# First down projection of a decoder trunk: two of its seven block products in the wide form, and their additions moved between engines

## The chip, the core and the metric

The program runs on one core of a Trainium2 chip. Five engines work side by side, each in the order in which its instructions were written: TensorE (PE in the profile, with its weight loads as PEld) multiplies, VectorE (DVE) and ScalarE (ACT) work element by element, GpSimd (POOL) here mostly issues transfers that add to what lies at the destination, and SyncE (SP) issues plain transfers. They wait for one another by semaphores. The metric is the device time of one execution in microseconds, as a median of several runs.

## The reference

The reference is one decoder layer on 512 tokens of 1024 channels, in float32:

```python
x = x + 0.5 * swiglu(rmsnorm(x, ffn1_norm), ffn1_wg, ffn1_wu, ffn1_wd)
x = x + hybrid_mixer(rmsnorm(x, mix_norm), w_in, ...)
x = x + 0.5 * swiglu(rmsnorm(x, ffn2_norm), ffn2_wg, ffn2_wu, ffn2_wd)
return rmsnorm(x, final_norm)

def swiglu(x, w_gate, w_up, w_down):
    return (silu(x @ w_gate) * (x @ w_up)) @ w_down     # 1024 -> 2816 -> 1024
```

The change lies in the first of the three lines, in its last matrix product: the hidden values (2816 by 512 tokens) times `w_down` (2816 by 1024), scaled by one half and added to x. The mixer (sparse attention beside a gated recurrence) and the second feed-forward are as before.

## The kernel before

Values lie transposed: channels over the 128 partitions, tokens along a row. A float32 operand is split in two tiles that TensorE takes at its fast rate: a rounded one, written by ScalarE, and the remainder (value minus rounded value), written by VectorE. A product w times t is then three matmuls: rounded w by rounded t, rounded w by remainder of t, remainder of w by rounded t. For weights the tiles are called `wh` and `wl`; for operands `ch` and `cl`.

The down projections are done by blocks with seven products in place of eight (the scheme of Strassen and Winograd). The 22 hidden tiles make 11 pairs: ten pairs lie in five tiles `a` and `b` of two hidden tiles each (`ha_103`, `hb_104` and so on in the profile, numbered n = 0 to 4), and the last pair is called "joined" (j = 10, operands `cx`). With tokens halved (`lo`, `hi`, 256 columns each) and output channels halved (four tiles of 128, m = 0 to 3), each of the seven products takes sums or differences of blocks on both sides. The order of the work is the list `steps` in `block_down`, 78 steps: the joined steps of products 1 and 2, product 1, product 2, product 5 and its joined step, product 6, product 3, product 7, product 4. A group in the text below is one n of a product, two steps, that is 16 pairs of (k tile, m).

Around each step hangs a table of tasks, keyed by the step's number: `unit` splits the weights of two steps (one ScalarE and one VectorE instruction of 1024 columns), `operand` splits the operand, `difference` makes a(hi) - b(hi) for product 7 (it is needed from step 23 on), `reduced` turns a(hi) into a(hi) - a(lo) by a ScalarE copy with the sign turned and a transfer of GpSimd that adds it, and `joined_sum` adds weight blocks of the joined pair. Weights of products 1, 2 and 4 come from memory into three raw buffers `wr` (a load can start when VectorE has read the buffer), those of the other products into `sm`, `s` and `sj`, to which GpSimd's transfers add further blocks. Since every engine runs its own list in order, a task that is listed late or waits holds up all that stands behind it on that engine.

PSUM, where TensorE's sums build up, has eight banks of 512 columns, in two tags of four: `mm` and `aux`. Products 1, 6, 7 and 4 add up in `mm`, one bank for each m, of which product 1 and 6 use all 512 columns and 7 and 4 the lower 256. Product 2 uses two `aux` banks, two m in a bank; products 5 and 3 share two others in the same way.

Products 1 and 6 (the constant `BROAD`) take the wide form: the operand tile holds the rounded values in its lower 256 columns and the remainder in its upper 256, so the two matmuls with the rounded weights are one of 512 columns, and the third one of 256 adds to the lower half. Per m and k tile these are two matmuls in place of three. The upper half of the bank has to be added at the end (`results1`). The operand takes two ScalarE and two VectorE instructions of 256 columns in place of one each of 512.

`results1(i)` adds a finished product's banks to x by one VectorE instruction of 256 columns for each m (`result1`). The tables are set by hand in steps; a later stage of the program has its order chosen by a planner (`Plan`). Line 251 in the profile is the helper that issues all arithmetic instructions, line 239 the one that issues transfers.

## Time and profile before

| | us |
|---|---|
| median of 3 runs | 1036.72 (1036.44 to 1037.26) |
| the profiled execution | 1036.25 |
| its span, first to last instruction | 1034.5 |
| TensorE busy in the span | 1027.6 (99%) |
| VectorE busy | 906.6 (88%) |
| ScalarE busy | 710.4 (69%) |
| GpSimd busy | 203.3 (20%) |
| granted TensorE clock | 0.999 |

The stage of the change lies from about 226 to 337 us of the span. By stretches of it: the first product without its joined step takes 13.97 us of TensorE, the second 14.40, the fifth and the third 15.84 each with their joined steps, the sixth 15.40. A time stands in us from the span's start. VectorE's and ScalarE's instructions are pipelined: a row's duration is longer than the distance to the next row's start, and where work is added up below, that distance is used.

### The profile page before, as it was taken

Reading aid. Unit: us, or ns where it says so; the run is one execution under the profiler, and the core shown is the slowest. Engines: PE = TensorE matmul, PEld = TensorE weight load, DVE = VectorE, ACT = ScalarE, POOL = GpSimd, SP = SyncE. Lnnn points to the kernel's source line nnn. Section 1 sums busy time; section 2 is a strip of 40 time slices with the busy share of each in tenths; the row PEclk is TensorE's granted clock in tenths of the full one; section 3 lists DMA queues with packets and bytes.
Section 4 is the critical chain, followed back from the end, with each engine's and each line's share of the span. In section 5 each row is a group of like instructions: output and inputs, shape, how many; then the busy total and the mean of one; then the engine's idle time right before and its main releaser. Section 6 shows DMA issues by size and latency. Waiting matters only on the chain.

```text
span 1034.5 us, 16004 instructions
## 1 busy us (share of the span) xinstructions
PE 1027.6 (99%) x5600; PEld 892.9 (86%) x5600; DVE 906.6 (88%) x1571; ACT 710.4 (69%) x1195; POOL 203.3 (20%) x255
## 2 busy tenths in 40 slices
PE   9999999999999999999999999999999999999997
PEld 8898888899999888888888888888988888898886
DVE  7988999889998888998989966777889999989886
ACT  8856766666766669978896674367666766657864
POOL 1613333213240011111101110013432333110000
PEclk9999999999999999999999999999999999999999
DMA  9969999897994463343469987793889999987564
GB/s 355 201 171 216 222 238 216 192 275 194 183 244 152 149 181 101 107 128 107 122 187 282 278 212 209 208 295 62 193 226 245 215 221 227 205 203 225 167 189 164
DMA packets 92257, 206.01 MB, mean 199 GB/s; under 512 B 18576, under 2 KB 25872, under 8 KB 92176
## 3 DMA queue, kind: packets, MB, share of 16 engines
q1 hardware_dynamic: 59952, 141.75, 41.0%
q0 software_dynamic: 31936, 62.93, 35.0%
q8 instruction: 44, 0.72, 0.3%
q10 hardware_dynamic: 288, 0.31, 0.1%
q14 instruction: 37, 0.30, 0.1%
HBM read 185.02 MB, written 25.17 MB: 203 GB/s over the span
## 4 chain that ended last, share of the span: by engine, by line
PE 99%; DVE 0%; DVEq 0%; issue 0%
PE mm L251 72%; PE aux L251 27%; PE aux L1340 0%; DVE xr L251 0%; DVE o L251 0%; DVE sq L251 0%; DVEq L2568 0%; DVE rs L251 0%; DVE ss L251 0%
## 5 line engine op out<-in xcount | busy, mean ns | idle before, releaser
L251 DVE TENSOR_TENSOR wl<-wr,wh 128x1024 fp32r<-128x1024 f32 (+3 forms) x154 | 183.0, 1189 | 30.6 <-ACT wh L251 30.1
L251 ACT ACTIVATE wh<-wr 128x1024 fp32r<-128x1024 f32 (+2 forms) x155 | 158.8, 1026 | 43.4 <-PE mm L251 20.0
L251 PE MATMUL mm<-cm,wh 128*128 128x512 f32 (+1 forms) x736 | 167.0, 354 | 0.0
L251 PEld LDWEIGHTS mm<-cm,wh 128*128 128x128 f32 x736 | 126.3, 190 | 15.8
L251 PE MATMUL mm<-yn,wh 128*128 128x512 f32 x420 | 130.8, 393 | 0.0
L251 PE MATMUL aux<-cm,wh 128*128 128x512 f32 (+1 forms) x472 | 119.5, 383 | 0.0
L251 PE MATMUL mm<-cm,wl 128*128 128x256 f32 x608 | 108.3, 282 | 0.0
L251 PEld LDWEIGHTS aux<-cm,wh 128*128 128x128 f32 x472 | 86.0, 188 | 15.6
L251 PEld LDWEIGHTS mm<-cm,wl 128*128 128x128 f32 x608 | 92.2, 190 | 4.7
L251 PEld LDWEIGHTS mm<-yn,wh 128*128 128x128 f32 x420 | 77.0, 188 | 14.8
L251 PE MATMUL mm<-yn,wl 128*128 128x512 f32 x210 | 81.9, 390 | 0.0
L251 PE MATMUL aux<-cm,wl 128*128 128x256 f32 x456 | 70.5, 282 | 0.0
L251 ACT ACTIVATE wh<-a 128x1024 fp32r<-128x1024 f32 (+1 forms) x68 | 57.1, 842 | 18.2 <-DVE a L251 17.2
L251 DVE TENSOR_TENSOR wl<-a,wh 128x1024 fp32r<-128x1024 f32 (+1 forms) x68 | 64.7, 952 | 5.5 <-ACT wh L251 5.0
L251 PE MATMUL mm<-yh,wh 128*128 128x512 f32 (+1 forms) x168 | 65.4, 392 | 0.0
L251 PE MATMUL mm<-yl,wh 128*128 128x512 f32 (+1 forms) x168 | 65.3, 390 | 0.0
L251 PEld LDWEIGHTS aux<-cm,wl 128*128 128x128 f32 x456 | 63.1, 191 | 1.9
L251 PE MATMUL mm<-yh,wl 128*128 128x512 f32 x160 | 62.1, 390 | 0.0
L251 ACT ACTIVATE tu<-mm 128x512 f32<-128x512 f32 (+1 forms) x57 | 28.2, 495 | 43.8 <-PE mm L251 43.7
L251 DVE TENSOR_TENSOR wl<-s,wh 128x1024 fp32r<-128x1024 f32 (+1 forms) x46 | 49.3, 1080 | 1.2 <-ACT wh L251 1.1
L251 ACT ACTIVATE wh<-s 128x1024 fp32r<-128x1024 f32 (+1 forms) x46 | 43.0, 943 | 7.1 <-PE mm L251 2.0
L251 PEld LDWEIGHTS mm<-yn,wl 128*128 128x128 f32 x210 | 39.4, 188 | 8.5
(400 smaller groups left out, 2596.8 us busy)
## 6 DMA issues: line engine op xcount, KB each, us to landing
wr<-wm SPq DMA_DIRECT2D x39, 512.0 KB, 3.6
w<-w2d SPq DMA_DIRECT2D x20, 512.0 KB, 7.0
wr<-w SPq DMA_DIRECT2D x20, 512.0 KB, 3.5
wr<-w1u SPq DMA_DIRECT2D x19, 512.0 KB, 5.9
s<-w2u SPq DMA_DIRECT2D x36, 256.0 KB, 4.4
wr<-w2u SPq DMA_DIRECT2D x18, 512.0 KB, 5.6
s<-w2u POOLq DMA_DIRECT2D x36, 256.0 KB, 6.3
s<-w1u SPq DMA_DIRECT2D x32, 256.0 KB, 4.8
```

Source lines behind the costliest of these rows:

```text
L251: return call(*args, **kw)
```

## The change

1. Products 5 and 3 take the wide form too (`BROAD`). They now have four `aux` banks, one for each m, and with that no bank is left beside the two of product 2: the banks of m = 2 and 3 are those that product 2 has to give back first. The first group of product 5 is therefore written in halves, m = 0, 1 for both of its steps and then m = 2, 3, and product 2's additions to x are listed ahead of it. Products 5 and 3 each need four more additions at their end (the upper halves). Product 5's and 3's operands are split by instructions of 256 columns.
2. `difference`, in this projection only, is a ScalarE copy of b(hi) with the sign turned and a transfer of GpSimd that adds a(hi); it was one VectorE subtraction. There are five.
3. The four `joined_sum` additions are listed at steps 12, 14, 16 and 18 (they were at 20 to 23).

```diff
--- before.py
+++ after.py
@@ -49,7 +49,7 @@
 PLAIN1, PAIRS1, TAIL, PLAIN2, PAIRS2, TAIL2 = 2, 10, 3, 2, 10, 4
 DIRECT, BEGIN = 2, 14
 SUMS_AT = -12, -11, -7, -5, -2
-BROAD = (1, 6)
+BROAD = (1, 6, 5, 3)
 WIDE, FIRST_FOLD = (2, 5, 3), 3
 KEPT, TURN = 6, 20
 MERGES = {(0, 0): 4, (1, 0): 7, (2, 1): 12, (3, 1): 16, (2, 0): 34, (3, 0): 36, (0, 1): 50, (1, 1): 54}
@@ -1117,7 +1117,11 @@
 
         def difference(n):
             ra[n] = two(slot(F32, "cr"))
-            V.tensor_sub(ra[n], a(n, hi), b(n, hi))
+            if made:
+                V.tensor_sub(ra[n], a(n, hi), b(n, hi))
+            else:
+                A.activation(ra[n], b(n, hi), AF.Copy, scale=-1.0)
+                G.dma_start(ra[n], a(n, hi), accum_op=ALU.add)
 
         def reduced(n):
             if made:
@@ -1195,7 +1199,7 @@
 
             for at, row in ((-9, 0), (-8, 1), (3, 2), (5, 3)):
                 task(at, [("SP", 0.6, lambda row=row: joined_load(row), False)])
-            for at, o, m, n in ((20, "w5", 2, 3), (21, 2, 2, 0), (22, 0, 0, "w5"), (23, 1, 1, 0)):
+            for at, o, m, n in ((12, "w5", 2, 3), (14, 2, 2, 0), (16, 0, 0, "w5"), (18, 1, 1, 0)):
                 task(at, lambda o=o, m=m, n=n: joined_sum(o, m, n))
 
         used = []
@@ -1492,17 +1496,18 @@
     broads1 = {}
 
     def chain1(p, m):
-        if CHAIN.get(p, p) == 1:
-            return broad1(m)[:, lo]
+        if p in BROAD or CHAIN.get(p, p) == 1:
+            return broad1(p, m)[:, lo]
         key = CHAIN.get(p, p), m // 2
         if key not in banks1:
             banks1[key] = psum("aux")
         return banks1[key][:, (lo, hi)[m % 2]]
 
-    def broad1(m):
-        if (1, m) not in broads1:
-            broads1[1, m] = psum()
-        return broads1[1, m]
+    def broad1(p, m):
+        key = CHAIN.get(p, p), m
+        if key not in broads1:
+            broads1[key] = psum("aux" if key[0] == 5 else "mm")
+        return broads1[key]
 
     def products1(i, ms=range(KD // 2)):
         if steps[i] is None:
@@ -1514,8 +1519,8 @@
             t = d1.turned[p, j]
             for m in ms:
                 c = slice(m * P, (m + 1) * P)
-                T.matmul(broad1(m), h[:, c], d1.whole[p], start=i == firsts1[1], stop=False, **opens)
-                T.matmul(broad1(m)[:, lo], l[:, c], t[0], start=False, stop=False, **opens)
+                T.matmul(broad1(p, m), h[:, c], d1.whole[p], start=i == firsts1[1], stop=False, **opens)
+                T.matmul(broad1(p, m)[:, lo], l[:, c], t[0], start=False, stop=i == lasts1[p], **opens)
             return
         if p in BROAD:
             h, l = d1.units[i // 2]
@@ -1524,9 +1529,9 @@
                 for m in ms:
                     c = slice(n % 2 * S + m * P, n % 2 * S + (m + 1) * P)
                     if j % 2 == 0:
-                        T.matmul(broad1(m), h[:, c], t, start=False, stop=False, **opens)
+                        T.matmul(broad1(p, m), h[:, c], t, start=p == 5 and n == 0, stop=False, **opens)
                     else:
-                        T.matmul(broad1(m)[:, lo], l[:, c], t[:, lo], start=False, stop=n == PAIRS1 - 1, **opens)
+                        T.matmul(broad1(p, m)[:, lo], l[:, c], t[:, lo], start=False, stop=n == PAIRS1 - 1 == lasts1[p] - i + j, **opens)
             return
         th, tl = d1.turned[p, j]
         for m in ms:
@@ -1550,13 +1555,13 @@
                     if st[0] == 6:
                         seconds = work("sq") if m % 2 == 0 else seconds
                         half_ = seconds[:, (lo, hi)[m % 2]]
-                        A.activation(half_, broad1(m)[:, hi], AF.Copy)
-                        V.tensor_add(broad1(m)[:, lo], half_, broad1(m)[:, lo])
+                        A.activation(half_, broad1(1, m)[:, hi], AF.Copy)
+                        V.tensor_add(broad1(1, m)[:, lo], half_, broad1(1, m)[:, lo])
                     result1(st[0], m, *a)
-                    if st[0] == 1:
+                    if st[0] in (1, 5, 3):
                         s_, half, sign = a
                         r = x[half * KD // 2 + m][:, (lo, hi)[s_]]
-                        V.scalar_tensor_tensor(r, broad1(m)[:, hi], 0.5 * sign, r, op0=ALU.mult, op1=ALU.add)
+                        V.scalar_tensor_tensor(r, broad1(st[0], m)[:, hi], 0.5 * sign, r, op0=ALU.mult, op1=ALU.add)
 
     def norm_round(k, c):
 
@@ -1587,14 +1592,17 @@
         plan.clear()
         cs = decay()
         turn_ = lasts1[7]
+        fifth_ = firsts1[5]
         for i in range(last):
-            if i in (turn_ - 1, turn_ + 1):
+            if i == fifth_:
+                results1(i - 1)
+            if i in (turn_ - 1, turn_ + 1, fifth_):
                 for ms in ((0, 1), (2, 3)):
-                    for k in (0, 1) if i < turn_ else (0, 2):
+                    for k in (0, 2) if i == turn_ + 1 else (0, 1):
                         products1(i + k, ms)
-            elif i not in (turn_, turn_ + 3):
+            elif i not in (turn_, turn_ + 3, fifth_ + 1):
                 products1(i)
-            if i and i - 1 != turn_:
+            if i and i - 1 not in (turn_, fifth_ - 1):
                 results1(i - 1)
             if i == turn_:
                 results1(i)
```

TensorE has 88 matmuls fewer, VectorE 13 instructions more, ScalarE 15 more, GpSimd five transfers more; SyncE's list is the same, and behind the projection the order on every engine is as before.

Where product 5 begins, TensorE had this before (`aux_2986` and `aux_2993` are the banks of product 5, m = 0 and 1 share the first; `ch` and `cl` the operand's rounded part and remainder, `wh` and `wl` those of the weights):

```order
L251 MATMUL aux_2986<-ch_2907,wh_2926 128x256
L251 MATMUL aux_2986<-cl_2908,wh_2926 128x256
L251 MATMUL aux_2986<-ch_2907,wl_2927 128x256
L251 MATMUL aux_2986<-ch_2907,wh_2926 128x256
L251 MATMUL aux_2986<-cl_2908,wh_2926 128x256
L251 MATMUL aux_2986<-ch_2907,wl_2927 128x256
```

and has this now (`aux_3003`, `aux_3005`, `aux_3013`, `aux_3015` are the banks of m = 0 to 3; `ch_2916` and `cl_2917` are the two k tiles of the group, each with both parts):

```order
L251 MATMUL aux_3003<-ch_2916,wh_2938 128x512
L251 MATMUL aux_3005<-ch_2916,wh_2938 128x512
L251 MATMUL aux_3003<-cl_2917,wh_2938 128x512
L251 MATMUL aux_3005<-cl_2917,wh_2938 128x512
L251 MATMUL aux_3003<-ch_2916,wl_2939 128x256
L251 MATMUL aux_3005<-ch_2916,wl_2939 128x256
L251 MATMUL aux_3003<-cl_2917,wl_2939 128x256
L251 MATMUL aux_3005<-cl_2917,wl_2939 128x256
L251 MATMUL aux_3013<-ch_2916,wh_2938 128x512
L251 MATMUL aux_3015<-ch_2916,wh_2938 128x512
L251 MATMUL aux_3013<-cl_2917,wh_2938 128x512
L251 MATMUL aux_3015<-cl_2917,wh_2938 128x512
```

Three matmuls of 256 columns became one of 512 and one of 256, ordered by halves of m; the ninth row is the first that needs a bank of product 2.

VectorE from the end of product 1's additions to x (`x<-mm`) to the weights of product 5 (`wl` from `sm`), before (`wl` from `wr` are the remainders of product 2's weights, groups 2, 3 and 4; `cl` are operands' remainders):

```order
L251 SCALAR_TENSOR_TENSOR x_95<-mm_2617,x_95 128x256 x2
L251 SCALAR_TENSOR_TENSOR x_95<-mm_2620,x_95 128x256 x2
L251 TENSOR_TENSOR wl_2822<-wr_2742,wh_2821 128x1024
L251 TENSOR_TENSOR cl_2838<-hb_110,ch_2837 128x512
L251 TENSOR_TENSOR wl_2857<-wr_2770,wh_2856 128x1024
L251 TENSOR_TENSOR cl_2873<-hb_112,ch_2872 128x512
L251 TENSOR_TENSOR wl_2892<-wr_2796,wh_2891 128x1024
L251 TENSOR_TENSOR cl_2908<-ha_103,ch_2907 128x512
L251 TENSOR_TENSOR wl_2927<-sm_2399,wh_2926 128x1024
L251 TENSOR_TENSOR cl_2943<-ha_105,ch_2942 128x512
L251 TENSOR_TENSOR sj_2959<-sj_2680,sj_2712 128x512
L251 TENSOR_TENSOR wl_2965<-sm_2408,wh_2964 128x1024
```

and now (`sj` are the joined sums, the pairs `ch_2916`, `cl_2917` the wide operand of product 5):

```order
L251 SCALAR_TENSOR_TENSOR x_95<-mm_2617,x_95 128x256 x2
L251 SCALAR_TENSOR_TENSOR x_95<-mm_2620,x_95 128x256 x2
L251 TENSOR_TENSOR sj_2823<-sj_2682,sj_2715 128x512
L251 TENSOR_TENSOR wl_2829<-wr_2746,wh_2828 128x1024
L251 TENSOR_TENSOR cl_2845<-hb_110,ch_2844 128x512
L251 TENSOR_TENSOR sj_2682<-sj_2682,sj_2448 128x512
L251 TENSOR_TENSOR wl_2865<-wr_2775,wh_2864 128x1024
L251 TENSOR_TENSOR cl_2881<-hb_112,ch_2880 128x512
L251 TENSOR_TENSOR sj_2448<-sj_2448,sj_2823 128x512
L251 TENSOR_TENSOR wl_2901<-wr_2801,wh_2900 128x1024
L251 TENSOR_TENSOR ch_2916<-ha_103,ch_2916 128x256
L251 TENSOR_TENSOR cl_2917<-ha_103,cl_2917 128x256
```

A joined sum stands ahead of each of product 2's last three weight remainders, and an operand of product 5 is two instructions of 256 columns.

ScalarE at the start of product 1, before (`wh` are rounded weights of product 1, `ch` and `cl` there the wide operands):

```order
L251 ACTIVATE tg_2360<-tg_2360 128x512
L251 ACTIVATE wh_2625<-wr_2519 128x1024
L251 ACTIVATE ch_2629<-ha_107 128x256
L251 ACTIVATE cl_2630<-ha_107 128x256
L251 ACTIVATE wh_2662<-wr_2552 128x1024
L251 ACTIVATE ch_2666<-ha_109 128x256
L251 ACTIVATE cl_2667<-ha_109 128x256
```

and now (`cr` are the differences for product 7):

```order
L251 ACTIVATE tg_2360<-tg_2360 128x512
L251 ACTIVATE cr_2623<-hb_104 128x512
L251 ACTIVATE wh_2626<-wr_2519 128x1024
L251 ACTIVATE ch_2630<-ha_107 128x256
L251 ACTIVATE cl_2631<-ha_107 128x256
L251 ACTIVATE cr_2661<-hb_106 128x512
L251 ACTIVATE wh_2664<-wr_2552 128x1024
L251 ACTIVATE ch_2668<-ha_109 128x256
L251 ACTIVATE cl_2669<-ha_109 128x256
```

One copy of 512 columns was put ahead of each weight of product 1. GpSimd's list in the same place:

```order
 L239 DMA sm_2516<-w1d 128x1024
+L239 DMA cr_2623<-ha_103 128x2x256
 L239 DMA sm_2574<-w1d 128x1024
-L239 DMA ha_103<-cr_2818 128x2x256
-L239 DMA ha_105<-cr_2853 128x2x256
-L239 DMA ha_107<-cr_2888 128x2x256
-L239 DMA ha_109<-cr_2923 128x2x256
+L239 DMA cr_2661<-ha_105 128x2x256
+L239 DMA cr_2694<-ha_107 128x2x256
+L239 DMA cr_2727<-ha_109 128x2x256
```

Five adding transfers of 128 by 512 values stand ahead of the five of `reduced` (`ha<-cr`); the first of them stands ahead of the last addition to product 5's weights (`sm_2574`).

## The prediction

> **What bounds the kernel now.** I read the busy times of the page first, then the chain of work that ended last, cut to the stretch of this projection, then the engines' rows in order of time around it.
>
> ```profile
> span 1034.5 us, 16004 instructions
> PE 1027.6 (99%) x5600; PEld 892.9 (86%) x5600; DVE 906.6 (88%) x1571; ACT 710.4 (69%) x1195; POOL 203.3 (20%) x255
> ```
>
> TensorE bounds the whole: 6.9 us of the span are not its own. So an edit pays only what it takes off TensorE's list, and costs whatever TensorE comes to wait for. The chain's pieces (start, us, count):
>
> ```profile
> 229.69 13.97 PE mm L251 x80
> 243.66 30.24 PE aux L251 x252
> 273.90 15.40 PE mm L251 x88
> 289.30 15.84 PE aux L251 x132
> 953.47 72.09 PE mm L251 x318
> ```
>
> The second row is products 2 (120 matmuls) and 5 (132), the third is the sixth in the wide form, the fourth is the third product. 30.24 / 252 = 0.120 us for a matmul of 256 columns, start to start; the last row gives 72.09 / 318 = 0.2267 us for 512 columns. There is no gap in products 2, 5 and 3, so TensorE waits for nothing there now. Product 2 runs from 243.66 to 258.06, product 5 to 273.90. A group of product 2 takes 24 x 0.120 = 2.88 us; its third group starts at 249.42.
>
> VectorE in the same stretch (start, us, idle before):
>
> ```profile
> 224.62 0.68 DVE L251 TENSOR_TENSOR cr<-ha,hb 128x512 f32<-128x512 f32 x1
> 243.05 1.23 DVE L251 TENSOR_TENSOR wl<-wr,wh 128x1024 fp32r<-128x1024 f32 x1 [1.23 <-ACT wh L251]
> 244.19 0.68 DVE L251 TENSOR_TENSOR cl<-hb,ch 128x512 fp32r<-128x512 f32 x1
> 244.79 3.24 DVE L251 SCALAR_TENSOR_TENSOR x<-mm,x 128x256 f32<-128x256 f32 x8
> 247.95 1.22 DVE L251 TENSOR_TENSOR wl<-wr,wh 128x1024 fp32r<-128x1024 f32 x1
> 249.08 0.68 DVE L251 TENSOR_TENSOR cl<-hb,ch 128x512 fp32r<-128x512 f32 x1
> ...
> 256.19 1.23 DVE L251 TENSOR_TENSOR wl<-sm,wh 128x1024 fp32r<-128x1024 f32 x1 [0.45 <-ACT wh L251]
> 257.34 0.68 DVE L251 TENSOR_TENSOR sj<-sj,sj 128x512 f32<-128x512 f32 x1
> 257.94 0.68 DVE L251 TENSOR_TENSOR cl<-ha,ch 128x512 fp32r<-128x512 f32 x1
> 258.54 1.41 DVE L251 SCALAR_TENSOR_TENSOR x<-aux,x 128x256 f32<-128x256 f32 x4
> 259.87 0.68 DVE L251 TENSOR_TENSOR sj<-sj,sj 128x512 f32<-128x512 f32 x1
> 269.29 0.41 DVE L251 TENSOR_TENSOR ch<-ha,ch 128x256 fp32r<-128x256 f32 x1
> 269.63 0.41 DVE L251 TENSOR_TENSOR cl<-ha,cl 128x256 fp32r<-128x256 f32 x1
> ```
>
> Two things are to be seen. The remainder of product 2's third group (the `wl` at 247.95) ends at 249.17, and TensorE uses it in the group's third matmul, at 249.42 + 0.24 = 249.66: half a microsecond of slack, though VectorE had stood idle for 1.23 us shortly before. And the additions of product 2 to x start at 258.54, half a microsecond after TensorE is done with it, because VectorE is behind its work. VectorE is the second bound, and it gets work here. From start to start its prices are 1.13 us for 1024 columns (247.95 to 249.08), 0.60 for 512 (257.34 to 257.94), 0.34 for 256 (269.29 to 269.63), 3.16 for eight additions and 1.33 for four (258.54 to 259.87).
>
> **The change part by part.** *Wide products.* Products 5 and 3 have 44 pairs each of m and k tile; per pair three matmuls of 256 columns (0.360 us) become one of 512 and one of 256 (0.347). By these prices a product takes 15.26 instead of 15.84, 0.58 less. The sixth, the same work in the same form, took 15.40, so the form gave 0.44. I take the measured row: 2 x 0.44 = 0.88 us gained, with 1.16 as the other end. (The Trainium skill, "TensorE: Matmul & The Clock Gate", section "Wait — 56ns, not 53.3ns?", puts the fixed cost of a warm matmul at about 2.5 ns beyond its columns. Here the row gives 13 ns at 256 columns, 120 against 256 / 2.4 = 106.7. By the page the 88 matmuls saved would be an estimate of 0.2 us; the trace decides.)
>
> *VectorE's list in product 2.* Now a joined sum stands ahead of each of the last three remainders of product 2, and a fourth ahead of product 5's first; before, all four came behind. I add up from 244.79, where the eight additions start: additions to 247.95, sum to 248.55, remainder of the third group from there, done at 249.77. Wanted at 249.66; with a handover of 0.05 (an estimate) TensorE is late by 0.15. On: operand and sum 1.20, remainder 1.13, operand and sum 1.20, remainder 1.13, so 254.34 (each in time: the fifth group starts at 255.18); then the first operand of product 5 in two pieces 0.68, sum 0.60, remainder 1.13, operand 0.68, remainder 1.13, operand 0.68, which is 259.24. VectorE has no idle time left in this stretch. Behind that come product 2's four additions.
>
> *The banks at the start of product 5.* TensorE is there at 258.21. It can do m = 0 and 1 for both steps at once, 4 x 0.2267 + 4 x 0.120 = 1.39 us, to 259.60. For m = 2 it needs the first bank of product 2, free after two of the additions: 259.24 + 0.75 + 0.05 = 260.04, a wait of 0.44. One matmul later, at 260.27, it needs the second, free at 259.24 + 1.41 + 0.05 = 260.70: 0.43 more. Queued behind this matmul is all of product 5. Together with the 0.15 the new waits are 1.02 us. Lower end: if VectorE were one 0.60 operation earlier, as it is where the differences were taken from it, 0.42; upper end: a further sum or operand late, 1.62.
>
> *Differences by ScalarE and transfers.* This takes 5 x 0.60 us off VectorE, but in the first product, where it ended in idle time: the wait of 1.23 us before 243.05 is for rounded weights. ScalarE and the transfers there:
>
> ```profile
> 241.96 1.06 ACT L251 ACTIVATE wh<-wr 128x1024 fp32r<-128x1024 f32 x1 [1.81 <-DMA wr<-w1d]
> 235.89 8.73 SPq L239 DMA_DIRECT2D wr<-w1d  x4
> wr<-w1d SPq DMA_DIRECT2D x1, 512.0 KB, 6.0
> ```
>
> The load issued at 235.89 landed 6.0 us later, at 241.9; that sets VectorE's 243.05 and with it the 244.79 from which I counted. ScalarE has room for five copies (8.17 us busy of 14.00 in this product, second row below), but the transfers do not have much (columns: PE, PEld, DVE, ACT, POOL busy, clock, share of the 16 DMA engines, GB/s):
>
> ```profile
> 229.00:233.00 4.00, 4.00 (x25) 3.56 (x25) 4.00 (x7) 1.67 (x3) 0.00 (x0) 1.00 0.95 232
> 229.70:243.70 14.00, 14.00 (x82) 12.32 (x82) 12.26 (x19) 8.17 (x13) 0.00 (x0) 1.00 0.85 267
> 233.00:237.00 4.00, 4.00 (x23) 3.43 (x22) 4.00 (x8) 2.12 (x4) 0.00 (x0) 1.00 0.81 303
> 237.00:241.00 4.00, 4.00 (x27) 3.62 (x26) 3.48 (x5) 2.72 (x4) 0.00 (x0) 1.00 0.83 253
> 249.00:253.00 4.00, 4.00 (x36) 4.00 (x35) 4.00 (x6) 2.88 (x4) 2.27 (x2) 1.00 0.77 114
> DMA to landing us min/median/max: 3.8/4.4/6.4
> ```
>
> The stretch 249 to 253 holds only the adding transfers of `reduced`, the same kind and size (the last row is their time from issue to landing): 0.77 x 4 = 3.08 us of all engines for 114 x 4 = 0.456 MB, or 1.74 transfers, 1.77 us each. Five new ones want 8.9 us of a stretch that has 0.05 x 4 + 0.19 x 4 + 0.17 x 4 = 1.6 us free from 229 to 241. They share the engines with the loads of product 2's weights; the load at 235.89 and the one before it in the same buffer each meet about one of them. If packets alternate, a load is held up by half of one, 0.9 us, twice 1.8; against that VectorE frees the buffers up to 0.6 earlier. So the delay X of VectorE's restart lies between 0 (the loads go past) and 1.2 (alternating); I take the middle, 0.6. It adds in full, since from there VectorE is never idle and both waits follow it.
>
> *What costs nothing.* The four extra additions of product 5 (1.33 us) fall into the sixth, where VectorE's remainder of the third group is early:
>
> ```profile
> 277.91 1.22 DVE L251 TENSOR_TENSOR wl<-sm,wh 128x1024 fp32r<-128x1024 f32 x1
> 308.08 1.28 DVE L251 TENSOR_TENSOR wl<-s,wh 128x512 fp32r<-128x512 f32 x2
> ```
>
> It is done at 279.13. A wide group takes 13.97 / 5 = 2.8 us, so the third one's is wanted at 273.90 + 1.39 (joined step) + 2 x 2.80 + 1.81 (its eight wide matmuls) = 282.7. Those of product 3 stand ahead of the 308.08, done at 309.36, wanted by the seventh's third group at 305.14 + 1.44 + 2 x 2.88 = 312.34. Without that cover each would cost up to 1.33. Operands in two pieces cost VectorE 0.08 a group, inside the same slack. The first difference's transfer stands ahead of the last addition to product 5's weights on GpSimd and delays it by some 2 us; it is used in product 5's last group, at 258.06 + 4 x 2.88 = 269.6.
>
> **Sum.** -0.88 + 1.02 + 0.60 = +0.74 us on the span, 1034.5 to 1035.2. The profiled execution was 1036.25, 1.75 around its span, and the median of the runs shown lies 0.47 above it: 1036.72 + 0.74 = 1037.5. From the ends: -1.16 + 0.42 = 1036.0, and -0.88 + 1.62 + 1.2 = 1038.7.
>
> **Rivals.** *The gain comes through whole*: VectorE, lightened early, is never late, the banks are free in time. For it speaks that products 1 and 6 run wide without a wait; against it the 0.5 us of slack that a 0.60 us sum is put into. Time: 1036.72 - 0.88 = 1035.8.
>
> *The adding transfers hold up the weights* (slower): if each load queues behind a whole adding transfer, both loads in the buffer's round are 1.77 late, less the 0.6: X = 2.9, and -0.88 + 1.02 + 2.9 = +3.1, 1039.8. For it: five times 1.77 us into 1.6 us of room. Against it: a load may fall between two transfers, which are issued some 3 us apart, one for each group of product 1. It decides from X = 1.9 on, where the time passes 0.2%. (The Trainium skill, "DMA: Bandwidth & Descriptors", section "Queues, rings and completion order", says that a DMA engine takes turns between queues a whole packet at a time, of some 9 to 17 descriptors; by that rule a load would stand behind the whole of an adding transfer's share on that engine. No run here shows it yet.)
>
> *The change moves nothing on TensorE*: the wide form's gain is not found in products that start from banks in use; then the waits alone stand, 1036.72 + 1.02 + 0.6 = 1038.3.
>
> **How the numbers follow.** 0.2% is 2.07 us, about what a measurement of this kernel tells from no change. The forecast gets 0.50 (its own range 1036.0 to 1038.7), the whole gain 0.22, the held-up weights 0.20, no gain on TensorE 0.05, and 0.03 stays for a shift in the later stages that brings over 2 us. From 1034.65 to 1038.79 lies no change: 0.48 of the forecast, the 0.22 and 0.04 of the last rival, 0.74 same; the 0.03 faster; 0.02 + 0.20 + 0.01 = 0.23 slower. The range takes in the second case and most of the third: 1035.3 to 1039.6.
>
> **What would show it.** In the profile after: products 5 and 3 at 15.3 to 15.5 us of matmuls; TensorE idle for about half a microsecond at each of two banks at the start of product 5, put down to VectorE's `x<-aux`; a short wait at product 2's third group for `wl`; `wr` loads of product 2 landing later than 6.0 us; VectorE with no idle between the first product's additions and the second's. The forecast is wrong if the fifth starts without a wait, or if TensorE waits for `wh<-wr` in product 1 or 2.

## The result, and the profile after

The changed kernel takes 1043.26 us, median of 6 runs (1042.85 to 1044.33), against 1036.59 for the kernel before beside it (1036.44 to 1037.26). The ratio is 1.0064, 95% interval 1.0051 to 1.0077: slower, by more than three times the 0.2% that a measurement tells apart, and above the upper end of the predicted range (1039.6). The page of the profiled execution, which took 1043.33 us:

```profile
span 1041.6 us, 15878 instructions
PE 1029.8 (99%) x5512; PEld 890.0 (85%) x5512; DVE 908.3 (87%) x1584; ACT 713.3 (68%) x1210; POOL 211.7 (20%) x260
PE 95%; DVE 3%; DMA 1%; issue 0%; ACT 0%; DVEq 0%; ACTq 0%
```

TensorE has 88 matmuls fewer and yet the span is 7.1 us longer. "Busy 99%" hides it: 11.8 us of the span are not TensorE's own, where it was 6.9. The chain of waits names the place. Before, it ran through TensorE alone from 229.69 on; now a part of it runs through a transfer (start, us, what):

```profile
236.20 10.40 DMA wr<-w1d
246.70 1.07 ACT wh L251
247.79 1.23 DVE wl L251
249.02 0.60 DVE cl L251
...
252.70 0.68 DVE sj L251
253.38 1.15 DVE wl L251
254.57 25.58 PE aux L251 x158
280.15 15.37 PE mm L251 x88
```

A load of product 2's weights takes 10.40 us (its counterpart before, issued at 235.89, took 6.0), ScalarE and VectorE stand behind it, and TensorE starts its next row of matmuls only at 254.57. What TensorE waited for between 226 and 350 us, by releaser (total, times, longest; the same view of before has no row):

```profile
PE aux L251 <- DVE wl L251: 3.5, 3, 2.4
PE mm L251 <- DVE x L251: 1.2, 1, 1.2
PE aux L251 <- ACT wh L251: 0.3, 1, 0.3
```

VectorE's rows show the same from its side (start, us, idle before; `...` stands where rows are left out):

```profile
239.78 1.23 DVE L251 TENSOR_TENSOR wl<-wr,wh 128x1024 fp32r<-128x1024 f32 x1 [2.94 <-ACT wh L251]
...
244.28 1.22 DVE L251 TENSOR_TENSOR wl<-wr,wh 128x1024 fp32r<-128x1024 f32 x1 [2.67 <-ACT wh L251]
...
247.79 1.23 DVE L251 TENSOR_TENSOR wl<-wr,wh 128x1024 fp32r<-128x1024 f32 x1 [1.69 <-ACT wh L251]
...
249.54 3.25 DVE L251 SCALAR_TENSOR_TENSOR x<-mm,x 128x256 f32<-128x256 f32 x8
252.70 0.68 DVE L251 TENSOR_TENSOR sj<-sj,sj 128x512 f32<-128x512 f32 x1
253.30 1.22 DVE L251 TENSOR_TENSOR wl<-wr,wh 128x1024 fp32r<-128x1024 f32 x1
```

The eight additions that started at 244.79 before start at 249.54: the delay X of the prediction is 4.75 us.

**A ledger that closes.** The waits above are only those that a row shows as idle. For a finer count I took, matmul by matmul from 226 to 350 us, the distance to the next one's start, and summed what lies above 0.120 us (256 columns) or 0.227 (512). Before, this sum is 0.78 us; after, 8.76. A span should then be 1034.5 plus the difference of the sums, less 0.88 where products 5 and 3 are wide: 1034.5 + 7.98 - 0.88 = 1041.6, the span measured. The same sum is used for every run below; I call it the lost time. The later stages of the program contribute hardly anything: from 350 to 1040 us they lose 6.6 us before and 6.8 after, so the ledger closes to about 0.2 us.

Of the 8.76 us, product 2 has 4.7 in waits (0.45 and 0.92 at its first steps, 0.53 at its second group, 2.52 at its third, and 0.1 behind each), 1.6 lie in the matmuls right behind the longest wait, and 1.32 are a single wait before product 4's joined step, at 326.5.

### The profile page after: what moved, and what is told of

It is laid out like the page before. It is cut to its first block, busy times and chain, and to the rows that moved or that the text cites. A ratio compares the mean times of both kernels' runs of the same rounds, so it can differ in the third digit from the quotient of the medians.

```text
span 1041.6 us, 15878 instructions
## 1 busy us (share of the span) xinstructions
PE 1029.8 (99%) x5512; PEld 890.0 (85%) x5512; DVE 908.3 (87%) x1584; ACT 713.3 (68%) x1210; POOL 211.7 (20%) x260
## 4 chain that ended last, share of the span: by engine, by line
PE 95%; DVE 3%; DMA 1%; issue 0%; ACT 0%; DVEq 0%; ACTq 0%
PE mm L251 68%; PE aux L251 26%; DMA wr<-w1d 1%; DVE wl L251 1%; DVE x L251 1%; PE aux L1344 0%; DVE cl L251 0%; ACT wh L251 0%; DVE ha L251 0%; DVE xr L251 0%; DVE o L251 0%; DVE acc L251 0%; DVE sq L251 0%; DVE yl L251 0%; DVE ch L251 0%
## 5 line engine op out<-in xcount | busy, mean ns | idle before, releaser
L251 PE MATMUL mm<-wh,cl 128*128 128x512 f32 (+1 forms) x120 | 46.3, 385 | 0.0
```

Of the source, the lines that this page charges most:

```text
L251: return call(*args, **kw)
```

## The experiments

Times stand beside those of the kernel before on the same chip: 1036.41 (25 runs) for `e1` to `e4`, 1036.61 (19) for `e5` to `e9`, 1036.72 (14) for `e10` to `e12`. In the expectations T is the theory that the adding transfers of the differences hold up product 2's weights; L, that the earlier joined sums stand ahead of weight remainders; B, that the wide form and its banks cost the time; S, that ScalarE's copies do.

### Differences back on VectorE (`e1_vsub`)

```diff
-            if made:
-                V.tensor_sub(ra[n], a(n, hi), b(n, hi))
-            else:
-                A.activation(ra[n], b(n, hi), AF.Copy, scale=-1.0)
-                G.dma_start(ra[n], a(n, hi), accum_op=ALU.add)
+            V.tensor_sub(ra[n], a(n, hi), b(n, hi))
```

> The changed kernel with the five differences back on VectorE (one subtraction each); wide products and early joined sums stay. Theory T (the five adding transfers fill the DMA engines in product 1, so that product 2's weights land late): the load that took 10.4 us lands in 5 to 6.5 us again, VectorE's additions of product 1 start at 244.5 to 245.5 us of the span, TensorE waits 0.2 to 1.2 us in products 2 and 5 together, and the time is 1036 to 1038. Rival L (the joined sums ahead of product 2's weights make VectorE late): most of the 6.7 us stays, 1041 or more. Rival B (the fifth product waits for banks in the wide form): 1040 or more, with the wait at the start of product 5.

Measured: 1038.21 us, ratio 1.0015 (1.0005 to 1.0025). About three quarters of the loss is gone: 5 of 6.7 us. That is 0.2 us above what T had, and far from the 1040 and more of L and B. Product 2's load is back at 5.5 us, and the additions start 0.13 us from where they did before. TensorE's rows at the start of product 5, and VectorE's where they begin:

```profile
244.92 3.25 DVE L251 SCALAR_TENSOR_TENSOR x<-mm,x 128x256 f32<-128x256 f32 x8
259.04 0.42 DVE L251 TENSOR_TENSOR cl<-ha,cl 128x256 fp32r<-128x256 f32 x1
259.38 1.42 DVE L251 SCALAR_TENSOR_TENSOR x<-aux,x 128x256 f32<-128x256 f32 x4
...
259.62 0.40 PE L251 MATMUL aux<-cl,wl 128*128 128x256 f32 x2
260.19 0.49 PE L251 MATMUL aux<-ch,wh 128*128 128x512 f32 x1 [0.17 <-DVE x L251]
260.85 0.50 PE L251 MATMUL aux<-ch,wh 128*128 128x512 f32 x1 [0.17 <-DVE x L251]
```

The two single wide matmuls are those of m = 2 and 3, each behind an addition of product 2; they cost 0.33 and 0.43 us of lost time, and 0.11 follows. Product 2's third group costs 0.32 + 0.10. So the waits that the prediction had worked out are there. But the lost time is 4.42 us, and about half of it is further on: 0.5 us in product 7 and, the largest part of all, 1.55 before product 4's joined step, the wait of 1.32 us that the changed kernel has too. VectorE there:

```profile
308.60 3.24 DVE L251 SCALAR_TENSOR_TENSOR x<-aux,x 128x256 f32<-128x256 f32 x8
...
321.57 1.22 DVE L251 TENSOR_TENSOR wl<-wr,wh 128x1024 fp32r<-128x1024 f32 x1
322.71 1.41 DVE L251 SCALAR_TENSOR_TENSOR x<-mm,x 128x256 f32<-128x256 f32 x4
```

The first row is product 3's additions, eight where there were four. Product 7's, which free the banks for product 4, start at 322.71. Before, they started at 320.25:

```profile
320.25 1.41 DVE L251 SCALAR_TENSOR_TENSOR x<-mm,x 128x256 f32<-128x256 f32 x4
```

They are 2.46 us later here, while TensorE, without the wait, would come to product 4's joined step only 0.97 us later (321.79, by the distances between its matmuls' starts, against 320.82). The stretch 302 to 322 us, before and here (VectorE's is the third busy time):

```profile
302.00:322.00 20.00, 20.00 (x169) 19.99 (x168) 18.15 (x33) 14.12 (x23) 3.88 (x6) 1.00 0.65 168
```

```profile
302.00:322.00 20.00, 19.90 (x154) 18.97 (x152) 19.86 (x37) 14.63 (x26) 8.05 (x8) 1.00 0.77 187
```

VectorE had 1.85 us left there before, and has 0.14 now: 18.15 against 19.86 of 20.

### The differences alone, and the copies alone (`e2_only_diff`, `e3_act_add`)

The first is the kernel before with only the second of the change's three parts. The second is the changed kernel with ScalarE's copies, but with VectorE adding in place of the transfer:

```diff
                 A.activation(ra[n], b(n, hi), AF.Copy, scale=-1.0)
-                G.dma_start(ra[n], a(n, hi), accum_op=ALU.add)
+                V.tensor_add(ra[n], ra[n], a(n, hi))
```

> The kernel before with nothing but the five differences by ScalarE copy and adding transfer. T: loads of product 2 land after 9 to 11 us, TensorE waits 3 to 6 us in product 2, 1040 to 1043. L and B: the sums and the wide form are as before, so within 0.5 us of 1036.6.

> The changed kernel with ScalarE's five sign-turned copies kept, but the addition made by VectorE in place of the transfer. T: the loads land as in the kernel before, 1036 to 1038. Rival S (the five copies in ScalarE's list hold up the rounding of the weights): TensorE still waits several us in product 2, 1041 or more.

Measured: the differences alone take 1041.29 us, ratio 1.0045 (1.0030 to 1.0060), with the waits of the changed kernel (0.41, 0.92, 0.52 and 1.93 us at the same four places, nothing at product 4). The copies without the transfers take 1038.70, ratio 1.0020 (1.0011 to 1.0030), 0.7 us above the upper end that T had, with 4.2 us of lost time at the places of `e1_vsub`. So it is the transfers, and not ScalarE's part, and they do their harm without the wide products and without the earlier sums.

### The wide products alone (`e4_wide_only`)

The differences on VectorE and the joined sums at steps 20 to 23, as before.

> The kernel before with products 5 and 3 in the wide form alone (differences on VectorE, joined sums at steps 20 to 23). T: TensorE saves 0.9 to 1.2 us and waits at the banks of product 5 for 0.5 to 1.5 us, 1035.5 to 1037.5. B: a wait of 3 us or more at product 5, 1039 or more. If the third product's four extra additions are what made the seventh's additions late, 1.0 to 1.5 us of waiting stands before product 4's joined step here too.

Measured: 1038.58 us, ratio 1.0020 (1.0011 to 1.0030). The wait at product 2's third group is gone, as L has it. The banks still cost 0.11 + 0.43 + 0.11 us at the start of product 5, product 3 has 0.45 us of new waits, and the wait before product 4's joined step is the same 1.48. So this wait belongs to the wide form itself, as the last sentence of the expectation had it, and the gain of 0.88 us is more than eaten by it. The time lies between T's and B's: the banks cost what T says, the rest comes from products 3, 7 and 4.

### Two of the five transfers, and fewer loads behind them (`e5_two`, `e6_no_sj`)

```diff
-            if made:
+            if made or n > 1:
                 V.tensor_sub(ra[n], a(n, hi), b(n, hi))
```

```diff
             def joined_load(row):
+                if row > 1:
+                    parts_[row] = parts_[row - 2]
+                    return
                 parts_[row] = slot(F32, "sj")
```

> The change, but with only the first two differences by copy and adding transfer, the other three by VectorE. Theory T (each adding transfer takes about half of the DMA engines' time while it runs, the loads behind it on SP's queue stand in line and their delays add up): with two of five transfers the slip of the load for product 2's first group falls from 4.8 us to about 2, little more than the 1.0 us that VectorE idles there in the kernel before, so the half-microsecond waits at product 2's first steps shrink below 0.5 in sum and the 2.5-us wait goes away; about 1039 us. Rival (one collision of one late transfer with one load does the harm): as after, waits of over 3 us between 243 and 255, if that one transfer is among the first two, or nothing at all if it is not.

> The change, but without the two loads of joined rows 2 and 3 that stand on SP's queue between product 2's weights; rows 0 and 1 are used in their place, so the joined parts of products 5, 3 and 4 are computed from other numbers and the output is not the reference's. Theory T with the queue (loads land in turn, so every load stands behind all that was delayed): the two loads are 256 KB each, 9.4 and 11.1 us from issue to landing in the changed kernel; without them the fourth weight load of product 2 lands 1.3 us earlier (two halves of a load's 1.3 us on the engines) up to 2.7 us earlier (each at half speed), so the 2.5-us wait at 251.9 falls to 0 to 1.2 us and the stretch at half clock behind it is gone; the waits at 243.7 and 244.5 stay at 0.4 and 0.9, since these loads are ahead of the joined ones. Rival (VectorE's four sums and their place, not the loads, hold up product 2): the waits stay as in the changed kernel, 2.5 us in sum at 251.9.

Measured, one run each: 1041.10 and 1040.28 us. Two transfers delay the additions from 244.92 to 247.17 (2.25 us, with 2.3 us of waits in product 2); five with two loads fewer, to 246.29 (1.4 us, with 2.0 of waits). The waits at product 2's first steps and at its third group:

| | additions start | waits at 243 to 246 | wait at the third group |
|---|---|---|---|
| differences on VectorE | 244.92 | 0 | 0.32 |
| five transfers, two loads fewer | 246.29 | 0.2 | 1.71 |
| two transfers | 247.17 | 0.6 | 1.57 |
| five transfers, all loads | 249.54 | 1.6 (and 0.6 at 248.4) | 2.52, and 1.6 at a slower clock |

The delay grows with the transfers, and with what is queued on SP ahead of a load: without the two loads of 256 KB, issued at 231.7 and 233.6 in the changed kernel, the load issued at 236 landed after 6.9 us, not 10.4. That is more than the 2.7 us that I allowed for. With two transfers the delay of 2.25 us is about the 2 expected, but it does more than expected: the third group still waits 1.57 us, and the time is 2 us above the 1039. The waits at product 2's first steps, which I had expected to stay, nearly went: the first joined load, issued at 231.7, stands ahead of the weights issued at 233.1 too. The third group's wait stayed above the 1.2 us expected: it follows the start of VectorE's additions, still 1.4 us late.

### Plain transfers in place of adding ones (`e12_plain`)

```diff
-                G.dma_start(ra[n], a(n, hi), accum_op=ALU.add)
+                G.dma_start(ra[n], a(n, hi))
```

> The change with the five adding transfers as plain transfers of the same bytes on the same queue: the first input overwrites the negated copy in place of being added to it, so the differences are wrong and the output is not the reference's. Theory A (it is the adding that is slow, 101 to 108 ns for each packet of 1 KB): the five transfers take half the engines' time or less, product 2's loads land in 5 to 6 us, the waits of 3.4 us in product 2 go, about 1038.5. Rival P (any transfer of small packets on a second queue shares the engines with the loads): loads of 7 to 10 us and waits of 3 us or more at 243 to 252 stay, 1041 to 1043.

Measured: 1040.70 us, one run, between the two theories. The third group waits 1.33 us, the other waits of product 2 are gone, and the additions start at 245.87: 0.95 us later than with the differences on VectorE (244.92), where the adding transfers made it 4.62. The loads issued from 228.7 to 233.3 us took 7.8 to 8.3 us, as the rival has it, the next one, at 238.9, only 4.0. The packets from 228 to 236 us (queue, packets, MB, share of the 16 engines; SP's loads are q1, GpSimd's transfers q0). Before, after, and with plain transfers:

```profile
q1 hardware_dynamic: 448, 1.45, 55.2%
q0 software_dynamic: 126, 0.45, 32.0%
```

```profile
q0 software_dynamic: 441, 0.83, 64.1%
q1 hardware_dynamic: 159, 0.59, 27.1%
```

```profile
q0 software_dynamic: 317, 1.07, 62.8%
q1 hardware_dynamic: 265, 1.00, 32.0%
```

In these 8 us the loads get 27% of the engines' time in place of 55%, and 0.59 MB in place of 1.45. But q0 carries two kinds of transfers here: the differences, and the additions to product 5's weights (`sm`), which add in all three kernels. The first difference stands ahead of the second of these, and so it landed at 236.63 in place of 231.59, in the midst of the loads. The packets from 233 to 235 us, before and after:

```profile
q1 hardware_dynamic: 217, 0.60, 82.7%
```

```profile
q0 software_dynamic: 88, 0.36, 97.0%
q1 hardware_dynamic: 17, 0.03, 4.1%
```

88 packets for 0.36 MB are packets of 4 KB, those of the weights; a difference adds in packets of 1 KB. So in these 2 us it was the delayed weights that kept the loads from the engines, not a difference. The price of each kind is read where q0 carries it alone: `ha<-cr` of `reduced`, the same kind as the differences (before, 248 to 250 us), adding weights (before, 229 to 230) and plain differences (this run, 236 to 238):

```profile
q0 software_dynamic: 381, 0.37, 117.9%
```

```profile
q0 software_dynamic: 47, 0.19, 96.4%
```

```profile
q0 software_dynamic: 77, 0.27, 36.2%
```

(A share can pass 100%, since packets overlap.) A megabyte costs the engines 1.179 x 2 / 0.37 = 6.4 us when a difference is added, 0.964 x 1 / 0.19 = 5.1 when weights are added, and 0.362 x 2 / 0.27 = 2.7 on the same queue without adding, about what SP's loads cost, 0.827 x 2 / 0.60 = 2.8. So it is the adding that is dear, and not the queue: the weights come from memory as the loads do, in packets of 4 KB where the loads have 4 and 2 KB, and the adding makes 2.8 into 5.1. The step from 5.1 to 6.4 goes with the smaller packets and with another source, the core's own memory. The harm that is left with plain transfers comes from their 1.3 MB in a stretch whose engines are full, and from the weights behind the first of them, which landed at 236.26 here too. No run separates these two.

### VectorE relieved at its two late places (`e8_tiles`, `e9_both`, `e11_halves`)

All three have the differences on VectorE. The first moves two norm tiles of the later stage (1.43 us of VectorE each) to later steps, the second also spreads the joined sums, the third also splits product 7's additions in two halves, of which one stands ahead of product 4's first remainder.

```diff
-        then1(index[7, 0] + (1, 4, 7, 9)[k], lambda k=k: y.append(norm_tile(k, V_GM)))
+        then1(index[7, 0] + (1, 4, 9, 12)[k], lambda k=k: y.append(norm_tile(k, V_GM)))
...
-            for at, o, m, n in ((12, "w5", 2, 3), (14, 2, 2, 0), (16, 0, 0, "w5"), (18, 1, 1, 0)):
+            for at, o, m, n in ((10, "w5", 2, 3), (10, 2, 2, 0), (20, 0, 0, "w5"), (40, 1, 1, 0)):
...
+            if i == turn_ - 1:
+                results1(turn_, (0, 1))
             if i == turn_:
-                results1(i)
+                results1(i, (2, 3))
```

> The change with differences on VectorE, and two of the four norm tiles (an addition to acc and a yl, 1.43 us of VectorE each) two and three steps later, so that one more of them stands behind product 7's additions. Theory V (from 302 to 322 us VectorE has no idle time, because of the 8 additions and 20 half operands that the wide products add, and product 7's additions are late by what is queued): the wait before product 4's joined step falls from 1.48 us to 0 to 0.2, the rest of the waits stay, time about 1036.8, the same as before within 0.1%. Rival W (the wait is for something else there, or the work moved comes back as a wait for product 4's second weights): a wait of 1 to 1.5 us stays between 321 and 330, time about 1038.2.

> As the last one, and the four joined sums spread: two at step 10, one at step 20, one at step 40, in place of steps 12 to 18. Theory L with V (product 2's third group waits for joined sums ahead of its weights' remainder, and product 5's banks wait because VectorE is behind by as much): the 0.32 us at 249.5 goes, the waits at the start of product 5 fall from 0.87 to 0.1 to 0.4 us, total of waits from 4.4 to about 1.5 us; time 1035.7, 0.7 us below the kernel before. Rival B (the banks wait is for the additions themselves, not for the backlog ahead of them): 0.8 us stays at product 5's start; 1036.4.

> The one before (differences on VectorE, joined sums spread, norm tiles later), and product 7's four additions in two halves: the first two already ahead of the remainder of product 4's first weights. Theory V (what is left of the wait before product 4's joined step, 0.29 us, is the 1.2 us of that remainder ahead of the additions): the wait goes, 1035.9. Rival (the remainder itself is then late): the 0.3 us comes back in product 4's first group, no change, 1036.2.

Measured:

| | us | ratio (interval) | lost time | third group of 2 | banks of 5 | product 4's joined step |
|---|---|---|---|---|---|---|
| differences on VectorE | 1038.21 | 1.0015 (1.0005 to 1.0025) | 4.42 | 0.42 | 0.87 | 1.55 |
| and norm tiles later | 1037.45 | 1.0009 (0.9999 to 1.0018) | 3.25 | 0.45 | 0.88 | 0.30 |
| and sums spread | 1036.18 | 1.0000 (0.9990 to 1.0009) | 1.80 | 0 | 0.05 | 0.29 |
| and additions in halves | 1036.45 | 0.9997 (0.9988 to 1.0006) | 1.46 | 0 | 0.05 | 0 |

The times are 0.5 to 0.65 us above those that the theory had (1036.8, 1035.7 and 1035.9), but each wait goes where the theory of a backlogged VectorE says, and against rival B the banks' wait vanishes with the backlog: with the sums spread, product 2's additions are in time and 0.05 us is left of 0.87. With halves, the wait before product 4's joined step is gone as well; the quarter of a microsecond did not show in the time: the profiled execution lost 7.6 us after 350 us where the one before it lost 6.6 (the one with the norm tiles alone lost 7.5 there). What is left of lost time, 1.46 against 0.78, nearly cancels the 0.88 gained. So the best form of the change ends where the kernel was: equal within 0.1%, not faster. The gain itself is real: by the matmuls' starts product 3 without its joined step takes 14.40 us before and 13.97 in `e9_both`, and products 2 and 5 together 28.80 and 28.41.

### The upper halves of product 3 added later (`e10_late`)

On top of the last one, product 3's four extra additions are taken from its end to product 4. Their terms then come after the first norm tiles have read x, so these tiles miss them.

```diff
-                    if st[0] in (1, 5, 3):
+                    if st[0] in (1, 5):
...
+    then1(index[7, 0] + 14, upper3)
```

> As the last one, and the four additions of product 3's upper halves (1.36 us of VectorE in all) not at product 3's end but in product 4, where VectorE has idle time. Theory V (the 0.4 us of waits in product 7 are for remainders that stand behind these four additions): they go, total of waits about 0.8 us as in the kernel before, and the 0.88 us of the wide products are left as gain: 1035.7, and under 0.2% below the kernel before (1036.6). Rival (the work comes back as a late remainder in product 4): a new wait of 0.5 to 1.4 us between 324 and 336, 1036.5.

Measured: 1049.97 us, ratio 1.0125 (1.0109 to 1.0141), which no theory had. In its own stretch it did as expected: between 261 and 341 us nothing over 0.05 us is left of the waits, those of product 7 included (a wait of 0.90 at product 2's third group is new: in this profiled execution the `sm` weights landed at 234.22, 2.4 us later than in the run with the halves, the load behind them 1.7 us later, and VectorE's additions started 1.4 us later; why the weights were late stays open). The time went in the mixer. TensorE there, with the halves alone and with the later additions:

```profile
627.00:660.00 33.00, 33.00 (x149) 27.31 (x148) 25.56 (x38) 13.03 (x19) 3.26 (x4) 1.00 0.73 195
```

```profile
627.00:660.00 33.00, 24.91 (x98) 18.68 (x97) 19.49 (x43) 15.83 (x30) 1.63 (x2) 0.84 0.39 106
```

8.1 of 33 us are idle, and the clock is 0.84. TensorE's written order in the planned stage is another one than in all other kernels here, whose orders agree there; so the loss is most likely the planner's, which got other costs and found a worse order. No run holds the order as it was, so that stays an argument.

## Why the prediction was wrong, point by point

*The wide products' gain, 2 x 0.44.* Right: 0.43 for product 3 and 0.39 for products 2 and 5, the latter with 0.05 of wait left in it, and the ledger closes with 0.88. The other end (1.16) was not reached.

*VectorE's list in product 2, 0.15.* Right in its mechanism, and too small: 0.32 us and 0.10 behind it, where the transfers don't disturb (`e1_vsub`); 0.13 of it is that the additions start at 244.92, not 244.79. The handover of 0.05 that the sum took without a row is what the changed kernel shows: the remainder ends at 254.52, TensorE starts at 254.57. It goes when the sums go elsewhere.

*The banks, 0.44 + 0.43.* Right: 0.33 + 0.43 + 0.11. In the changed kernel itself they don't appear, since TensorE, held up in product 2, comes to product 5 so late that the banks are free: product 2's additions start at 264.67 and the matmul of m = 2 at 265.96. So X and the banks' waits don't add up, as the sum had it.

*Transfers, X = 0.6.* This is the step that failed most. "If packets alternate, a load is held up by half of one, 0.9 us, twice 1.8" took each load by itself. X is 4.75. The loads on SP's queue landed in the order of issue, at 238.6, 241.2, 243.1, 244.6 and 246.6 us in the changed kernel, 2.1, 4.1, 4.6, 5.5 and 4.8 us later than before, so a delay was handed on to the next: the weights issued at 231.3, 233.1 and 236.2 took 7.3, 10.0 and 10.4 us, in place of 5.4, 5.0 and 6.0. The rows for it were in the prediction: 8.9 us of transfers into 1.6 us of room. A stretch overfilled by 7.3 us can hardly delay a load by only 0.6. And something stood under "what costs nothing" that did cost: that the first difference delays the last addition to product 5's weights "by some 2 us". It was 5.0 us, no harm to product 5, but the addition then took 97% of the engines from 233 to 235 us, where the loads had had them. By the load issued at 231.3 the delay was 2.1 us; how much of X this makes, no run separates. The rival "the adding transfers hold up the weights" named the mechanism, was given 0.20, and its 2.9 us was still too little, for the same reason: it counted two transfers, not all that stands in the queue. The rule of the Trainium skill that stood beside it, "DMA: Bandwidth & Descriptors", section "Queues, rings and completion order", that an engine takes turns between queues, spoke on the right side; the shares 64.1% and 27.1% agree with turns in which the adding queue holds the engine longer, though no run here shows the turns themselves.

*What costs nothing.* This failed too. The extra additions of product 3 were compared with the next weight remainder, wanted 3 us later. With the differences on VectorE that slack was used up: the remainder started at 312.36, 4.28 us later than before (308.08), and TensorE waited 0.2 us for it. The work queued behind it, up to product 7's additions to x, had less slack still. From 302 to 322 us VectorE had 1.85 us free. The four additions of product 3 took nearly all of it (x8 in 3.24 us there, x4 in 1.41 before), and it came into this stretch already late, by the four additions of product 5 and ten groups of operands in two pieces at 0.08. "Without that cover each would cost up to 1.33": it did, 1.55 before product 4's joined step and 0.5 in product 7. In the changed kernel this is the wait of 1.32 us. With these two and the other terms as forecast the time would have been 1037.5 + 2.0 = 1039.5, at the upper edge of the range.

*The sum.* Forecast +0.74 on the span, measured +7.1: 4.7 in product 2's waits in place of the 0.75 of X and the third group (4.0 more), 1.6 from a slow clock that no term had, 1.3 from product 4's joined step, less 0.9 for banks that didn't wait. That is 6.0 of the 6.4 between; the rest is in small pieces. Both signs of a wrong forecast came true: "if TensorE waits for `wh<-wr` in product 1 or 2", at 243.7 us, and "if the fifth starts without a wait".

## What to carry to other kernels

Before work is moved from an engine to transfers, add up the DMA engines' time in that very stretch with the transfers' own price, and if it overflows, follow the queue of loads to its end: here the delays of loads on one queue added up, and the last one decided. Ask too what a new transfer pushes back on its own queue: here it was an addition of 512 KB, pushed into the loads' stretch. Before extra work is put on an engine that is 88% busy, follow its list not to the next instruction with slack but to the next one that frees something, and count the idle time up to there; here 1.85 us of idle were not enough. A gain of 0.1% on the bounding engine is worth only what the second engine can afford.

## What the runs showed of the hardware that was not expected

Behind the longest wait TensorE ran at half its clock. The matmuls around the wait, and the stretches with their granted clock (the number behind the five busy times) in the changed kernel:

```profile
251.93 0.28 PE L251 MATMUL aux<-cl,wh 128*128 128x256 f32 x1
254.57 0.58 PE L251 MATMUL aux<-ch,wl 128*128 128x256 f32 x1 [2.36 <-DVE wl L251]
254.95 0.42 PE L251 MATMUL aux<-ch,wh 128*128 128x256 f32 x1
255.17 0.42 PE L251 MATMUL aux<-cl,wh 128*128 128x256 f32 x1
```

```profile
243.70:254.50 10.80, 7.09 (x53) 6.28 (x51) 8.40 (x15) 8.38 (x13) 3.18 (x3) 1.00 1.03 257
254.50:258.00 3.50, 3.43 (x16) 3.43 (x17) 3.50 (x7) 0.95 (x3) 1.67 (x2) 0.51 0.67 98
```

A matmul of 256 columns then takes 0.214 us from start to start in place of 0.120, for 3.4 us. This wait and those ahead of it had left TensorE busy for 7.09 of 10.80 us. With the differences alone, a wait of 1.93 us after the same three smaller ones left the clock at 1.00:

```profile
254.50:258.00 3.50, 3.50 (x32) 3.50 (x31) 3.50 (x5) 2.19 (x4) 1.22 (x1) 1.00 0.76 112
```

So the wait of 2.5 us cost 1.6 us more than itself, and the one of 1.93 did not. The length of a single wait alone does not decide it: in the run with the later additions the clock fell to half a second time, from 651.53 us on, behind waits of 1.20 and 0.93 us. The next rows show the 3.4 us (as long as the slow stretch in the changed kernel) ahead of each of these two falls, and the 3.4 us up to the end of the wait of 1.93 us, which left the clock at 1.00:

```profile
251.10:254.50 3.40, 1.11 (x10) 0.91 (x8) 3.33 (x8) 3.23 (x5) 1.98 (x2) 1.00 1.14 230
648.10:651.50 3.40, 1.27 (x4) 0.52 (x4) 2.11 (x6) 2.83 (x6) 0.00 (x0) 1.00 0.00 0
250.00:253.40 3.40, 1.65 (x14) 1.45 (x13) 3.30 (x8) 3.12 (x5) 1.59 (x2) 1.00 1.10 237
```

TensorE was busy for 1.11 and 1.27 us of these where the clock fell, and for 1.65 where it stayed. That fits a rule on the share of idle time; three stretches don't give its threshold.
